# Three transfers per attention head, forget gates kept on chip, and a fifth weight buffer in a hybrid streaming block

## The chip, the cores and the metric

The kernel runs on one core of one Trainium2 chip. The metric is the device time of one execution in microseconds (us). A core has a matrix engine (TensorE, PE in the profile, its weight loads PEld), a vector engine (VectorE, DVE), an activation engine (ScalarE, ACT), a general engine (GpSimd, POOL), a queue engine that here only issues transfers (SyncE, SP), and 16 DMA engines that move the data between the chip's memory (HBM) and the on-chip SBUF. Each engine runs its own instructions strictly in order and waits for the others by semaphores.

## What is computed

One residual block over 1024 tokens of width 1024, float32 throughout. Three token mixers work on one combined projection: HGRN2, a gated linear recurrence; FoX, a forgetting attention; and cross-attention into 256 memory tokens. The branches are gated, summed and projected out; a ConvGLU feed-forward follows. Cut to the parts that the change touches:

```python
h = rmsnorm(x); z = h @ W_in              # one projection, split by columns
# HGRN2, 4 heads of 128x128
f = lb + (1 - lb) * sigmoid(f_logit)      # forget gate, per channel and token
G = cumsum(log(f)) inside chunks of 64    # the decays
# FoX, 8 heads of 64, blocks of 128 queries
s = (q . k) / 8 + Fc[t] - Fc[s]           # Fc = cumsum(log_sigmoid(f_head))
o = softmax(mask(s)) @ v
# merge
y = sum_b sigmoid(gate_b) * (branch_b @ W_b);  x += y @ W_out
x += (gelu(conv3(a)) * v) @ W_down
```

## The kernel before

**Matrix products.** Every float32 product is made of three products of a higher and a lower part (`mm3`: high x high on L122, high x low on L123, low x high on L124). Large products are split further into seven products of sums of quarter blocks, so that each weight quarter is read once ("raw" piece), summed, split into parts and used. TensorE therefore has one long queue of matmuls on 128x512 tiles.

**Stages.** The memory keys and values come first, then the token-major part of the projection in stages 0 to 4; then the column-major units. `cm_unit` (L808) is one unit: it loads four raw weight pieces of 128x512 (256 KB each, tile `ur`, 4 buffers), forms sums on GpSimd (`us`, L758), splits each operand on ScalarE (`uh`, L752) and VectorE (`ul`, L753), and multiplies in seven steps. Units 0 to 5 give the HGRN2 forget gate, query and output gate of the four heads, and units 6 to 17 the merge gates. `fill_steps` (L981) runs all units as a generator, one step at a time, and the branch projections (L860) after them.

**Attention.** `fox_attn(h)` (L1027) is one of eight heads, also a generator. `weave` (L57) runs it together with a few steps of the fill (`FOX_FILL`), so that TensorE has fill matmuls while softmax is computed elsewhere. `fox_load(h)` (L1012) loads for a head:
- `kh` and `kl`, the key's high and low part: 64 channels in rows 0 to 63 and the same again in rows 64 to 127;
- `qa`, the query: its two parts in rows 0 to 63 and rows 64 to 127;
- `nf`, two halves of the decay row, broadcast to 128 rows; and `vhl`, the values, 512 KB.

Each of kh, qa and kl comes in two transfers of 64 rows of 4 KB, from the scratch tensors `kqd`, which stage 4 stored shortly before. All of these are issued on SyncE's queue. For head h > 0 the loads may issue only after the first output store of head h-1 (`marks["head"]`, L1029 and L1094); kh, qa and kl have one buffer for each parity of the head. The logits of a block are two matmuls, qa x kh (L1046) and qa x kl (L1047); VectorE adds the decay and takes the maximum (L1052), ScalarE takes the exponential (L1062), GpSimd scales (L1064), TensorE transposes (L1075 to L1078), and the product with the values (`po`, L1087 and L1088) is folded on ScalarE and VectorE (`yp`, L1091 and L1092), which frees the output bank, and stored (L1093).

**Forget gates and decays.** `put_hg` (L787) finishes the gate of an HGRN2 head in two halves: tanh on ScalarE, clamping on GpSimd, and a store to `hgd` on GpSimd's queue (L798). `decays(h)` (L963) loads the gate of a head again (`fk`, L966), scales it into two rows (L969 and L970), takes one Ln over 128x2048 on ScalarE (L972, with a table load of its own), and runs four cumulative scans (L975) with four subtractions (L976) on VectorE; then the two results are stored (L979). Its three steps run at steps 2, 4 and 6 of units 1, 2, 4 and 5.

**Order.** The program is written in the order of these generators; a scheduler with a modelled timeline then orders each engine's instructions. `tc.high_priority(n)` lets a piece go ahead of what was written before, `tc.issue_after(x)` keeps a piece behind instruction x.

Of the kernel before, what the change touches and what calls it, by code (L numbers as in the profile page):

```python
# [9 lines left out]
F32 = mybir.dt.float32  # L10
F32R = mybir.dt.float32r
AF = mybir.ActivationFunctionType
# [19 lines left out]
FOX_FILL = [2, 6, 5, 5, 5, 5, 5, 5]  # L32
HGRN_FILL = [32, 30, 28, 22]
AHEAD = 300
STAGE_STEPS = 3
ORDER = (1, 2, 0)
UNITS = [[("f", 0), ("q", 0)], [("g", 0), ("f", 1)], [("q", 1), ("g", 1)], [("f", 2), ("q", 2)],
# [32 lines left out]
def tile_block(ctx: ExitStack, tc: tile.TileContext, xT, x_rows, memT, vec, fbias, mats, hmask, w_ff, w_tm, w_cm,  # L70
# [679 lines left out]
    def u_operand(src):  # L750
        h, l = (ur.tile([P, HB], F32R, tag=t, name=t, bufs=3) for t in ("uh", "ul"))
        marks["cast"] = S.copy(h, src)  # L752
        V.tensor_sub(l, src, h.bitcast(F32))  # L753
        return h, l

    def u_sum(a, b):
# [19 lines left out]
    def put_gate(i):  # L776
# [7 lines left out]
            S.dma_start(gd[i, n], t)  # L784
        return put

    def put_hg(what, h):  # L787
        def put(c, n, ps, e):
            t = out_tile()
            dst = hgd[h][what][:, n * HB:(n + 1) * HB]  # L790
            if what == 0:
                if e is None:
                    S.activation(t, ps, AF.Tanh, scale=-0.5)
                else:
                    combine(t, ps, e, c)
                    S.activation(t, t, AF.Tanh, scale=0.5)
                G.tensor_scalar(t, t, TMIN, TMAX, ALU.max, ALU.min)
                G.dma_start(dst, t)  # L798
                return
            else:  # L800
                z = e if e is not None else ur.tile([P, HB], F32, tag="ue", name="ue", bufs=3)
                combine(z, ps, e, c)
                S.activation(t, z, AF.Tanh, scale=0.5)
                V.scalar_tensor_tensor(out=t, in0=t, scalar=1.0, in1=z, op0=ALU.add, op1=ALU.mult)
            SP.dma_start(dst, t)
        return put

    def cm_unit(u, puts):  # L808

        x, z, y = (banks[(u + i) % 3] for i in range(3))  # L810

        def put(c, n, ps, e):
            puts[c](c, n, ps, e)

        raw = []
        for i in range(4):
            t = ur.tile([P, HB], F32, tag="ur", name="ur", bufs=4)
            SP.dma_start(t, w_cm[u, i])
            raw.append(t)
        a11, a12, a21, a22 = raw  # L820
        o1, o6 = u_operand(a11), u_operand(a12)
        s1 = u_sum(a21, a22)
        s2 = u_sum(s1, a11)
        u_product(x, o1, "B11", True)
        e1 = u_snap(x)
        yield
        u_product(z, o6, "B21", True)
        put(0, 0, z, e1)
        o3 = u_operand(s2)
# [30 lines left out]
    def branches():  # L860
# [1 line left out]
        yh, yl = ([half[k // 2][:, k % 2, :] for k in range(4)] for half in halves)  # L862

        def chunk(br, j):
            raw = ur.tile([P, HB], F32, tag="ur", name="ur", bufs=4)
            SP.dma_start(raw, w_br[br, j])
            wh, wl = u_operand(raw)
            half = [slice(n * HB, (n + 1) * HB) for n in range(2)]

            def step(ps, n, k):  # L870
                ks = slice(k * P, (k + 1) * P)
                mm3(ps, wh[:, ks], wl[:, ks], yh[k][:, half[n]], yl[k][:, half[n]], k == 0, k == 3)

            if j in (0, 7):
                ps = [ps_proj(), ps_proj()]
                for k in range(4):
                    for n in range(2):
# [84 lines left out]

    def decays(h):  # L963

        fk = pf.tile([P, 2, T], F32, tag="fk", name=f"fk_{h}")
        SP.dma_start(fk[:, 0, :], hgd[h][0])  # L966
        yield
        hc = slice(h, h + 1)
        V.tensor_scalar(fk[:, 1, :], fk[:, 0, :], nc1[:, hc], c1p[:, hc], ALU.mult, ALU.add)  # L969
        V.tensor_scalar(fk[:, 0, :], fk[:, 0, :], c1[:, hc], c0[:, hc], ALU.mult, ALU.add)  # L970
        with tc.issue_after(marks["cast"].ins):
            S.activation(fk, fk, AF.Ln)  # L972
        for n in range(4):
            sl = slice(n * 256, (n + 1) * 256)
            V.tensor_tensor_scan(fk[:, 0, sl], resets, fk[:, 0, sl], 0.0, ALU.mult, ALU.add)  # L975
            V.tensor_sub(fk[:, 1, sl], fk[:, 0, sl], fk[:, 1, sl])  # L976
        yield
        for i in range(2):
            SP.dma_start(hgd[h][3 + i], fk[:, i, :])  # L979

    def fill_steps():  # L981
        for u, spec in enumerate(UNITS):
            for i, _ in enumerate(cm_unit(u, [puts_of(*s) for s in spec])):
                if u == len(UNITS) - 1 and i == 1:
                    load_y(ORDER[0])
                if u == 3 and i == 4:
                    recurrence_masks()
                if u in (1, 2, 4, 5):
                    if i == 2:
                        steps = decays((1, 2, 4, 5).index(u))  # L990
                    if i in (2, 4, 6):
                        next(steps, None)
                yield
        yield from branches()
        ur.release()
# [10 lines left out]
    resets = pf.tile([P, 256], F32, tag="resets", name="resets")  # L1006
    SP.dma_start(resets, mats[:, 3 * P:3 * P + 256])
    mskf = pf.tile([P, P], F32, tag="mskf", name="mskf")
    with tc.high_priority(2 * AHEAD):
        SP.dma_start(mskf, mats[:, 2 * P:3 * P])  # L1010

    def fox_load(h):  # L1012
        p, a = h // 2, slice(64 * (h % 2), 64 * (h % 2) + 64)
        kh, qa, kl = (pf.tile([P, T], F32R, tag=f"{t}{h % 2}", name=f"{t}_{h}") for t in ("kh", "qa", "kl"))
        for t, (u, v) in ((kh, (0, 0)), (qa, (2, 3)), (kl, (1, 1))):
            SP.dma_start(t[0:64, :].bitcast(F32), kqd[p][u // 2][a, u % 2, :])
            SP.dma_start(t[64:128, :].bitcast(F32), kqd[p][v // 2][a, v % 2, :])
# [9 lines left out]
    def fox_attn(h):  # L1027
# [3 lines left out]
        for tp in range(4):  # L1031
            pts = []
            for j in range(2):
                tb = 2 * tp + j
                ns = (tb + 1) * P
                tsl = slice(tb * P, (tb + 1) * P)
                pt = pf.tile([P, T], F32, tag="pt", name="pt", bufs=4)
                st = small("st", 4)
                nfm = pf.tile([P, P], F32, tag="nfm", name="nfm")
                G.tensor_tensor(nfm, nf[tb // 4][:, tb % 4 * P:tb % 4 * P + P], mskf, ALU.add)  # L1040
                m = 0
                for s0 in range(0, ns, HB):
# [851 lines left out]
```

## Time and profile before

| | |
|---|---|
| median of 3 runs | 1677.19 us (1676.16 to 1678.06) |
| the profiled execution | 1679.46 us, span 1677.7 us, mean granted clock 0.998 |
| TensorE busy | 1654.1 us, 99% of the span |
| VectorE, ScalarE, GpSimd busy | 1215.9, 845.5, 441.4 us |
| moved by DMA | 298.20 MB, 178 GB/s on average |
| first load of head 0 issued | 322.28 us |
| first logits of head 0 and of head 7 | 329.62 and 627.82 us |

The span runs from the first to the last instruction of the profiled execution, and its own time is some 2 us longer. In a row of a timeline stand start, duration, engine, line and operation, the tile written and the tile read, the shapes, and in brackets how long the engine stood idle before it and what ended that. "SPq" is an instruction that issues a transfer: its time is that of the issue, not of the transfer. In a row of the waits stand the engine with tile and line that waited, what it waited for, the total in us, how often, and the longest. In a row by stretches stand the stretch, its length, the busy time of PE, PEld, DVE, ACT and POOL with the number of instructions, the granted TensorE clock (1.00 is full), the share of the 16 DMA engines in use, and GB/s. "DMA packets" counts the pieces of the transfers, with the number of those under 512 B, 2 KB and 8 KB.

### The profile page before, as it was taken

To read this page: it belongs to the slowest core of one execution; us is meant where nothing else is said; L and a number is where in the kernel's file an instruction comes from. 1 tells how busy PE (TensorE), PEld (TensorE's weight loads), DVE (VectorE), ACT (ScalarE), POOL (GpSimd) and SP (SyncE) were. 2 spreads that over 40 slices of the span, in tenths; PEclk is the share of its full clock that TensorE was granted. 3 is DMA by queue.
4 is the path that set the end of the run, shared out by engine and by line. 5 is a ranking of instruction groups with operands and counts; after the bars stand their busy time and mean duration, and the time that the engine had idled before them with its cause. 6 is when DMAs were issued, how large, how long until landed. Compare 5 with 4: busy or idle time off the path is not lost.

```text
span 1677.7 us, 24989 instructions
## 1 busy us (share of the span) xinstructions
PE 1654.1 (99%) x8915; PEld 1417.1 (84%) x8915; DVE 1215.9 (72%) x2179; ACT 845.5 (50%) x1453; POOL 441.4 (26%) x469
## 2 busy tenths in 40 slices
PE   8999999999999999999999999999999999999999
PEld 7989999777788888888888888888888888888887
DVE  7875766588786766678776868978878788675664
ACT  8655554466666565556333257544434434343332
POOL 1143543455444444223011052221111111100000
PEclk9999999999999999999999999999999999999999
DMA  7253352655455552646866899666544454394782
GB/s 283 98 189 103 130 180 107 200 191 164 157 164 154 151 157 103 200 133 217 317 183 174 253 215 224 175 190 179 146 132 126 153 149 130 133 390 150 239 283 87
DMA packets 132061, 298.20 MB, mean 178 GB/s; under 512 B 14008, under 2 KB 31672, under 8 KB 131296
## 3 DMA queue, kind: packets, MB, share of 16 engines
q1 hardware_dynamic: 100576, 210.08, 36.9%
q0 software_dynamic: 22144, 71.84, 16.8%
q10 hardware_dynamic: 9216, 14.68, 2.3%
q8 instruction: 70, 1.15, 0.3%
q14 instruction: 55, 0.45, 0.1%
HBM read 216.40 MB, written 103.22 MB: 191 GB/s over the span
## 4 chain that ended last, share of the span: by engine, by line
PE 54%; DMA 1%; DVE 0%; ACT 0%; issue 0%
PE pp L122 10%; PE pp L123 10%; PE pp L124 10%; PE lg L124 4%; PE lg L122 4%; PE lg L123 4%; PE tr L122 3%; PE tr L124 3%; PE tr L123 3%; PE po L124 1%; PE po L122 1%; PE po L123 1%; DMA yd<-hz 1%; PE lg L1194 1%; PE lg L1185 0%; PE po L1227 0%
## 5 line engine op out<-in xcount | busy, mean ns | idle before, releaser
L1374 ACT CAST wh<-s 128x512 fp32r<-128x512 f32 x84 | 51.5, 620 | 119.1 <-PE pp L123 62.5
L128 ACT CAST dwh<-wr 128x1024 fp32r<-128x1024 f32 (+1 forms) x41 | 40.2, 980 | 114.9 <-PE tr L123 39.2
L1527 POOL DMA_DIRECT2D rw<-in_w_up x40 | 21.8, 551 | 260.5 <-DVE wl L1375 165.1
L752 ACT CAST uh<-ur 128x512 fp32r<-128x512 f32 x78 | 48.2, 618 | 77.7 <-PE pp L123 67.0
L1374 ACT CAST wh<-rw 128x512 fp32r<-128x512 f32 x66 | 40.6, 622 | 77.2 <-PE pp L123 47.2
L1064 POOL TENSOR_SCALAR pt<-pt,st 128x128 f32<-128x128 f32 (+3 forms) x64 | 57.5, 900 | 57.8 <-DVE st L1063 37.9
L136 DVE TENSOR_TENSOR dwl<-wr,dwh 128x1024 fp32r<-128x1024 f32 (+1 forms) x41 | 46.3, 1129 | 34.4 <-ACT dwh L128 34.3
L1062 ACT ACTIVATE pt<-pt,st 128x128 f32<-128x128 f32 (+3 forms) x64 | 49.8, 778 | 41.7 <-DVE st L1059 36.2
L753 DVE TENSOR_TENSOR ul<-us,uh 128x512 fp32r<-128x512 f32 x72 | 54.4, 759 | 21.5 <-ACT uh L752 21.0
L122 PE MATMUL pp<-B21h,uh 128*128 128x512 f32 x168 | 66.6, 398 | 1.2 <-DVE ue L150 1.2
L753 DVE TENSOR_TENSOR ul<-ur,uh 128x512 fp32r<-128x512 f32 x78 | 62.3, 800 | 6.0 <-ACT uh L752 5.1
L124 PE MATMUL pp<-B21h,ul 128*128 128x512 f32 x168 | 66.2, 394 | 0.1
L123 PE MATMUL pp<-T2l,uh 128*128 128x512 f32 x168 | 66.3, 395 | 0.0
L758 POOL TENSOR_TENSOR us<-ur 128x512 f32<-128x512 f32 x36 | 50.9, 1413 | 58.2 <-DMA ur<-in_w_cm 44.4
L122 PE MATMUL pp<-T2h,uh 128*128 128x512 f32 x168 | 66.1, 396 | 0.0
L123 PE MATMUL pp<-B21l,uh 128*128 128x512 f32 x168 | 65.9, 392 | 0.0
L124 PE MATMUL pp<-T2h,ul 128*128 128x512 f32 x168 | 65.8, 392 | 0.0
L752 ACT CAST uh<-us 128x512 fp32r<-128x512 f32 x72 | 43.9, 615 | 37.0 <-POOL us L758 21.1
L136 DVE TENSOR_TENSOR wl<-raw,wh 128x1024 fp32r<-128x1024 f32 x29 | 40.0, 1386 | 27.5 <-ACT wh L128 27.3
L758 POOL TENSOR_TENSOR us<-us,ur 128x512 f32<-128x512 f32 x36 | 49.5, 1375 | 38.7 <-issue 33.7
L1375 DVE TENSOR_TENSOR wl<-s,wh 128x512 fp32r<-128x512 f32 x84 | 57.3, 683 | 0.9 <-ACT wh L1374 0.6
L1375 DVE TENSOR_TENSOR wl<-rw,wh 128x512 fp32r<-128x512 f32 x66 | 44.4, 686 | 15.8 <-PE pp L124 13.5
(745 smaller groups left out, 6154.5 us busy)
## 6 DMA issues: line engine op xcount, KB each, us to landing
rw<-in_w_up POOLq DMA_DIRECT2D x40, 512.0 KB, 4.8
ur<-in_w_cm SPq DMA_DIRECT2D x72, 256.0 KB, 3.7
sd<-in_w_dn POOLq DMA_DIRECT2D x30, 512.0 KB, 8.3
br<-yd SPq DMA_DIRECT2D x30, 512.0 KB, 5.1
gd<-uo ACTq DMA_DIRECT2D x48, 256.0 KB, 3.0
gt<-gd SPq DMA_DIRECT2D x48, 256.0 KB, 5.0
yd<-fc SPq DMA_DIRECT2D x44, 256.0 KB, 2.3
raw<-in_w_tm SPq DMA_DIRECT2D x20, 512.0 KB, 3.4
```

Source lines behind the costliest of these rows:

```text
L122: PE.matmul(ps, lh, rh, start=first, stop=False, skip_group_check=more)
L123: PE.matmul(ps, lh, rl, start=False, stop=False, skip_group_check=more)
L124: return PE.matmul(ps, ll, rh, start=False, stop=last, skip_group_check=more)
L128: S.copy(out, in_)
L136: return (sub or V).tensor_sub(l, src, h.bitcast(F32))
L752: marks["cast"] = S.copy(h, src)
L753: V.tensor_sub(l, src, h.bitcast(F32))
L758: G.tensor_add(t, a, b)
L1062: S.activation(pt[:, :ns], pt[:, :ns], AF.Exp, bias=st[:, 2:3], accum_out=st[:, 3:4])
L1064: G.tensor_scalar(pt[:, :ns], pt[:, :ns], st[:, 3:4], 0.0, ALU.mult, ALU.add)
L1374: late["cast"] = S.copy(h, src)
L1375: late["split"] = V.tensor_sub(l, src, h.bitcast(F32))
```

## The change

It does seven things.
1. kh, kl and qa come in one transfer each, of 128 rows: for kh and kl the source is a broadcast of 2 over 64 rows of 4 KB, for qa the two parts are the outer dimension.
2. Head 0's three transfers get a high priority, and the load of `mskf` and one store of the HGRN2 query (`stored_late`) are kept behind them.
3. The raw weight tile `ur` has 5 buffers instead of 4.
4. The forget gates of heads 2 and 3 and the first half of head 1's are written straight into the `fk` tile and neither stored nor loaded. Head 0's gate and the second half of head 1's are still stored and loaded, in halves.
5. `decays` is split into steps at the places of a table (`DECAYS`): scaling, Ln, two scans, two scans and the first half of the stores, the rest of the stores. The scans are held behind the latest VectorE split (`marks["low"]`).
6. `pt` has a tile of its own size for each place of a block pair instead of 4 buffers of full width.
7. `nfm` has 2 buffers instead of 1.

```diff
+DECAYS = {at: (h, i == 0) for h, when in enumerate(((6, 8, 9, 10, 11, 12), (14, 16, 17, 18, 19, 20), (27, 28, 29, 30, 31), (35, 36, 37, 38, 39)))
+          for i, at in enumerate(when)}
...
     def put_hg(what, h):
         def put(c, n, ps, e):
-            t = out_tile()
+            kept = what == 0 and (h > 1 or (h == 1 and n == 0))
+            if kept:
+                if h not in gates:
+                    gates[h] = gate_tile(h)
+                t = gates[h][:, 0, n * HB:(n + 1) * HB]
+            else:
+                t = out_tile()
...
-                G.dma_start(dst, t)
+                if not kept:
+                    G.dma_start(dst, t)
...
-            SP.dma_start(dst, t)
+            if (what, h, n) == (1, 0, 1):
+                stored_late.append(partial(SP.dma_start, dst, t))
+            else:
+                SP.dma_start(dst, t)
...
-            t = ur.tile([P, HB], F32, tag="ur", name="ur", bufs=4)
+            t = ur.tile([P, HB], F32, tag="ur", name="ur", bufs=5)
...
     def decays(h):
-        fk = pf.tile([P, 2, T], F32, tag="fk", name=f"fk_{h}")
-        SP.dma_start(fk[:, 0, :], hgd[h][0])
+        if h == 0:
+            gates[h] = gate_tile(h)
+        fk = gates[h]
+        half = [slice(n * HB, (n + 1) * HB) for n in range(2)]
+        for n in ((0, 1), (1,), (), ())[h]:
+            SP.dma_start(fk[:, 0, half[n]], hgd[h][0][:, half[n]])
...
-        for n in range(4):
-            sl = slice(n * 256, (n + 1) * 256)
-            V.tensor_tensor_scan(fk[:, 0, sl], resets, fk[:, 0, sl], 0.0, ALU.mult, ALU.add)
-            V.tensor_sub(fk[:, 1, sl], fk[:, 0, sl], fk[:, 1, sl])
         yield
-        for i in range(2):
-            SP.dma_start(hgd[h][3 + i], fk[:, i, :])
+        for n in range(2):
+            for sl in (slice(n * HB + i * 256, n * HB + i * 256 + 256) for i in range(2)):
+                with tc.issue_after(marks["low"].ins):
+                    V.tensor_tensor_scan(fk[:, 0, sl], resets, fk[:, 0, sl], 0.0, ALU.mult, ALU.add)
+                V.tensor_sub(fk[:, 1, sl], fk[:, 0, sl], fk[:, 1, sl])
+            if n:
+                store(0)
+            yield
+        store(1)
...
-        for t, (u, v) in ((kh, (0, 0)), (qa, (2, 3)), (kl, (1, 1))):
-            SP.dma_start(t[0:64, :].bitcast(F32), kqd[p][u // 2][a, u % 2, :])
-            SP.dma_start(t[64:128, :].bitcast(F32), kqd[p][v // 2][a, v % 2, :])
+        twice = lambda part: kqd[p][0][a, part, :].unsqueeze(0).to_broadcast([2, 64, T])
+        with nullcontext() if h else tc.high_priority(2 * AHEAD):
+            for t, src in ((kh, twice(0)), (qa, kqd[p][1][a].rearrange("a b t -> b a t")), (kl, twice(1))):
+                loaded = SP.dma_start(t.bitcast(F32), src)
+        if h == 0:
+            with tc.high_priority(2 * AHEAD), tc.issue_after(loaded.ins):
+                SP.dma_start(mskf, mats[:, 2 * P:3 * P])
+            with tc.issue_after(loaded.ins):
+                stored_late.pop()()
...
-                pt = pf.tile([P, T], F32, tag="pt", name="pt", bufs=4)
+                pt = pf.tile([P, (5 + 2 * (tp % 2) + j) * P], F32, tag=f"pt{tp % 2}{j}", name="pt")
                 st = small("st", 4)
-                nfm = pf.tile([P, P], F32, tag="nfm", name="nfm")
+                nfm = pf.tile([P, P], F32, tag="nfm", name="nfm", bufs=2)
```

Lines move by 2 to 42: L1016 and L1017 become L1054, L1046 and L1047 become L1088 and L1089, L1092 becomes L1134, L975 becomes L1011.

SyncE's queue at the loads of head 0, before (kqd is the scratch tensor with keys and queries, hgd that of the recurrence, uo an output tile of a unit):

```order
95 L655 DMA kqd_96<-ko 256x1x512
96 L805 DMA hgd_101<-uo 128x512
97 L1010 DMA mskf<-in_mats 128x128
98 L1016 DMA kh_3820<-kqd_93 64x1024
99 L1017 DMA kh_3820<-kqd_93 64x1024
100 L1016 DMA qa_3821<-kqd_93 64x1024
101 L1017 DMA qa_3821<-kqd_93 64x1024
102 L1016 DMA kl_3822<-kqd_93 64x1024
103 L1017 DMA kl_3822<-kqd_93 64x1024
104 L1020 DMA nf<-negFd 128x512 x2
105 L1022 DMA vhl<-vhd_97 128x8x128
```

The same place after the change:

```order
95 L657 DMA kqd_96<-ko 256x1x512
96 L1054 DMA kh_3818<-kqd_93 128x1x1024
97 L1054 DMA qa_3819<-kqd_93 128x1x1024
98 L1054 DMA kl_3820<-kqd_93 128x1x1024
99 L1057 DMA mskf<-in_mats 128x128
100 L1059 DMA hgd_101<-uo 128x512
101 L1062 DMA nf<-negFd 128x512 x2
102 L1064 DMA vhl<-vhd_97 128x8x128
```

The three loads moved ahead of the store and the mask; each has 128 rows on the side of SBUF.

TensorE's queue at the first logits of head 0, before (pp is the bank of a fill product, lg that of the logits):

```order
2243 L1046 MATMUL lg<-kh_3820,qa_3821 128x128
2244 L1046 MATMUL lg<-kh_3820,qa_3821 128x256
2245 L122 MATMUL pp<-T1h,uh 128x512
2246 L123 MATMUL pp<-T1l,uh 128x512
2247 L122 MATMUL pp<-T2h,uh 128x512
2248 L123 MATMUL pp<-T2l,uh 128x512
2249 L124 MATMUL pp<-T2h,ul 128x512
2250 L122 MATMUL pp<-T2h,uh 128x512
2251 L123 MATMUL pp<-T2l,uh 128x512
```

And after:

```order
2242 L126 MATMUL pp<-B21h,ul 128x512
2243 L1088 MATMUL lg<-kh_3818,qa_3819 128x128
2244 L1088 MATMUL lg<-kh_3818,qa_3819 128x256
2245 L124 MATMUL pp<-T1h,uh 128x512
2246 L125 MATMUL pp<-T1l,uh 128x512
2247 L1089 MATMUL lg<-kl_3820,qa_3819 128x128
2248 L1089 MATMUL lg<-kl_3820,qa_3819 128x256
2249 L124 MATMUL pp<-T2h,uh 128x512
```

The kl products moved up by 13 rows: they are rows 2247 and 2248 now, four behind the first kh product, and were rows 2260 and 2261.

VectorE's queue at the decays of the third recurrence head, before (fk is the gate, yp the output half of a block pair, pl the lower part of the transposed weights of the softmax):

```order
505 L969 TENSOR_SCALAR fk_5911<-fk_5911,nc_71,c1p 128x1024
506 L1063 RECIPROCAL st<-st 128x1
507 L970 TENSOR_SCALAR fk_5911<-fk_5911,c_70,c_69 128x1024
508 L753 TENSOR_TENSOR ul<-us,uh 128x512
509 L975 SCALAR_TENSOR_TENSOR fk_5911<-resets,fk_5911 128x256 x4
510 L1092 TENSOR_TENSOR yp<-po,yp 64x256
```

And the decays of the same head after:

```order
472 L1002 TENSOR_SCALAR fk_5285<-fk_5285,nc_71,c1p 128x1024
473 L1105 RECIPROCAL st<-st 128x1
474 L1003 TENSOR_SCALAR fk_5285<-fk_5285,c_70,c_69 128x1024
475 L823 SCALAR_TENSOR_TENSOR uo<-uo,ue 128x512
476 L1094 ISA pt,st<-lg,nf 128x512
477 L1094 ISA st 128x1
478 L1134 TENSOR_TENSOR yp<-po,yp 64x256
479 L1094 ISA pt,st<-lg,nf 128x384
480 L1094 ISA st 128x1
481 L1094 ISA pt,st<-lg,nfm 128x128
482 L1094 ISA st 128x1
483 L1011 SCALAR_TENSOR_TENSOR fk_5285<-resets,fk_5285 128x256 x2
```

The addition into yp stands ahead of the scans now, and the four scans, one row before, are three rows now, 483, 486 and 488, with other work between.

More of the change, by code (lines that the diff above doesn't have):

```diff
@@ L752, in u_operand @@
         marks["cast"] = S.copy(h, src)
-        V.tensor_sub(l, src, h.bitcast(F32))
+        marks["low"] = V.tensor_sub(l, src, h.bitcast(F32))
         return h, l
@@ L785, in put_gate, with gate_tile @@
         return put
+    stored_late = []
+    gates = {}
+    def gate_tile(h):
+        return pf.tile([P, 2, T], F32, tag="fk", name=f"fk_{h}")
     def put_hg(what, h):
         def put(c, n, ps, e):
-            t = out_tile()
+            kept = what == 0 and (h > 1 or (h == 1 and n == 0))
[5 more added lines that the diff above has]
+                t = out_tile()
             dst = hgd[h][what][:, n * HB:(n + 1) * HB]
             if what == 0:
-                if e is None:
+                if kept and e is not None:
+                    combine(e, ps, e, c)
+                    S.activation(t, e, AF.Tanh, scale=0.5)
+                elif e is None:
                     S.activation(t, ps, AF.Tanh, scale=-0.5)
@@ L864, in chunk @@
         def chunk(br, j):
-            raw = ur.tile([P, HB], F32, tag="ur", name="ur", bufs=4)
+            raw = ur.tile([P, HB], F32, tag="ur", name="ur", bufs=5)
             SP.dma_start(raw, w_br[br, j])
@@ L963, in decays, with store @@
     def decays(h):
-        fk = pf.tile([P, 2, T], F32, tag="fk", name=f"fk_{h}")
-        SP.dma_start(fk[:, 0, :], hgd[h][0])
+        if h == 0:
[4 more added lines that the diff above has]
+            SP.dma_start(fk[:, 0, half[n]], hgd[h][0][:, half[n]])
+        if h < 2:
+            yield
+        hc = slice(h, h + 1)
+        def store(n):
+            for i in range(2):
+                SP.dma_start(hgd[h][3 + i][:, half[n]], fk[:, i, half[n]])
+        with tc.issue_after(marks["low"].ins):
+            V.tensor_scalar(fk[:, 1, :], fk[:, 0, :], nc1[:, hc], c1p[:, hc], ALU.mult, ALU.add)
+        V.tensor_scalar(fk[:, 0, :], fk[:, 0, :], c1[:, hc], c0[:, hc], ALU.mult, ALU.add)
         yield
-        hc = slice(h, h + 1)
-        V.tensor_scalar(fk[:, 1, :], fk[:, 0, :], nc1[:, hc], c1p[:, hc], ALU.mult, ALU.add)
-        V.tensor_scalar(fk[:, 0, :], fk[:, 0, :], c1[:, hc], c0[:, hc], ALU.mult, ALU.add)
         with tc.issue_after(marks["cast"].ins):
             S.activation(fk, fk, AF.Ln)
-        for n in range(4):
-            sl = slice(n * 256, (n + 1) * 256)
-            V.tensor_tensor_scan(fk[:, 0, sl], resets, fk[:, 0, sl], 0.0, ALU.mult, ALU.add)
-            V.tensor_sub(fk[:, 1, sl], fk[:, 0, sl], fk[:, 1, sl])
         yield
-        for i in range(2):
-            SP.dma_start(hgd[h][3 + i], fk[:, i, :])
+        for n in range(2):
+            for sl in (slice(n * HB + i * 256, n * HB + i * 256 + 256) for i in range(2)):
+                with tc.issue_after(marks["low"].ins):
+                    V.tensor_tensor_scan(fk[:, 0, sl], resets, fk[:, 0, sl], 0.0, ALU.mult, ALU.add)
+                V.tensor_sub(fk[:, 1, sl], fk[:, 0, sl], fk[:, 1, sl])
+            if n:
+                store(0)
+            yield
+        store(1)
     def fill_steps():
@@ L987, in fill_steps @@
                     recurrence_masks()
[L988 to L992, printed above, removed]
+                at = 7 * u + i
+                if at in DECAYS:
+                    h, begin = DECAYS[at]
+                    if begin:
+                        steps = decays(h)
+                    next(steps, None)
                 yield
@@ L1008, in tile_block @@
     mskf = pf.tile([P, P], F32, tag="mskf", name="mskf")
-    with tc.high_priority(2 * AHEAD):
-        SP.dma_start(mskf, mats[:, 2 * P:3 * P])
     def fox_load(h):
```

## The prediction

> **What bounds the kernel now.** The page first, for which engine fills the span.
>
> ```profile
> span 1677.7 us, 24989 instructions
> PE 1654.1 (99%) x8915; PEld 1417.1 (84%) x8915; DVE 1215.9 (72%) x2179; ACT 845.5 (50%) x1453; POOL 441.4 (26%) x469
> ```
>
> TensorE is busy for 99% of the span and the change leaves its matmuls alone, so all there is to win is its idle time, some 24 us, and what it loses at a low clock. All there is to lose is new idle time. The list of waits says where the idle time is; these are the rows of the stage that the change touches (attention woven with the column units, from about 320 us).
>
> ```profile
> engine line waited for: us in total, times, longest us
> PE po L1087 <- DVE yp L1092: 3.4, 1, 3.4
> PE lg L1047 <- DMA kl<-kqd: 1.8, 2, 1.0
> ...
> PE lg L1046 <- DMA qa<-kqd: 1.6, 1, 1.6
> ...
> PE tr L1075 <- POOL pt L1064: 0.5, 1, 0.5
> ```
>
> So 3.4 us in two or three waits for the head loads, and one wait of 3.4 us for VectorE. Of that last one the timelines of VectorE, ScalarE and TensorE tell the cause, read in this order.
>
> ```profile
> 425.13 1.28 ACT L972 ACT_TABLE_LOAD   x1
> 427.50 1.92 ACT L972 ACTIVATE fk<-fk 128x2048 f32<-128x2048 f32 x1 [1.08 <-DVE fk L970]
> ...
> 429.44 2.44 DVE L975 TENSOR_TENSOR_SCAN fk<-resets,fk 128x256 f32<-128x256 f32 x4 [1.38 <-ACT fk L972]
> 431.80 0.39 DVE L1092 TENSOR_TENSOR yp<-po,yp 64x256 f32<-64x256 f32 x1
> ...
> 432.34 0.55 PE L1087 MATMUL po<-ph,vhl 128*128 128x256 f32 x1 [3.41 <-DVE yp L1092]
> 432.69 0.63 PE L122 MATMUL pp<-B22h,uh 128*128 128x512 f32 x1
> 433.12 0.63 PE L123 MATMUL pp<-B22l,uh 128*128 128x512 f32 x1
> ```
>
> VectorE stood still 1.38 us for the Ln, then ran four scans, and the small addition that frees the output bank was queued behind them. The two matmuls after it start 0.43 us apart; elsewhere the same form starts 0.23 us apart (below). The table by stretches has the clock.
>
> ```profile
> 430.90:437.80 6.90, 5.46 (x14) 4.35 (x14) 5.63 (x12) 3.57 (x7) 1.12 (x1) 0.51 0.54 197
> 437.80:441.00 3.20, 3.20 (x22) 2.92 (x21) 3.00 (x7) 2.09 (x4) 2.60 (x3) 1.00 0.04 14
> ```
>
> At 0.51 from 430.9 to 437.8 us, the restart at 432.34 is followed by 5.4 us at half clock: 2.7 us lost on top of the 3.4. A long stall costs about 2.7 us more than its length here.
>
> **Part 1: the head loads.** Three transfers of 128 rows take the place of six of 64 rows, eight times. SyncE's timeline at head 1 has the old issue times, and TensorE's has the first use.
>
> ```profile
> 357.49 0.55 SPq L1016 DMA_DIRECT2D kh<-kqd  x1
> ...
> 360.00 0.59 SPq L1016 DMA_DIRECT2D kl<-kqd  x1
> 360.63 0.60 SPq L1017 DMA_DIRECT2D kl<-kqd  x1
> ...
> 367.28 0.30 PE L1047 MATMUL lg<-kl,qa 128*128 128x128 f32 x1 [0.96 <-DMA kl<-kqd]
> ```
>
> What the new transfers take is the disputed price. The new source of kh and kl is a leading dimension of 2 with stride zero over 64 rows of 4 KB, that of qa 2 by 64 rows with a real stride; the built program carries these patterns as [2, 64, 1024], while every old half had 64 in front. Two transfers of the trace show how many of the 16 DMA engines take part: a store of 8 rows alone in its window, and a load of 128 rows alone in its own.
>
> ```profile
> DMA packets 16, 0.03 MB, mean 9 GB/s; under 512 B 8, under 2 KB 8, under 8 KB 16
> ffd<-ff SPq DMA_DIRECT2D x1, 32.0 KB
> ```
> ```profile
> GB/s 0 0 0 0 0 0 0 0 0 0 0 0 164 131 33 66 66 33 33 66 131 328 360 426 426 393 426 360 459 295 1 0 0 0 0 0 0 0 0 0
> DMA packets 144, 0.26 MB, mean 105 GB/s; under 512 B 16, under 2 KB 16, under 8 KB 144
> ...
> ur<-in_w_cm SPq DMA_DIRECT2D x1, 256.0 KB
> ```
>
> Beside its data packets each transfer has packets under 512 B, one for each engine that reports its end: 16 for the 128 rows, 8 for the 8 rows. The trace thus bears out that the slowest dimension caps the number of engines at 8 when it is 8. It can't tell that from "8 packets, so at most 8 engines", since the eight rows were one packet each; no row has few rows in front and many packets. I take the cap to hold for 2 as well: two engines move each of the 24 transfers, one for each half.
>
> The Trainium skill speaks against this edit as much as for it. "DMA: Bandwidth & Descriptors", section "Rules for kernel authors", says that two transfers to disjoint halves of the partitions share the same engines and should be one of 128 partitions, which would make every load quicker. The same table warns that an outermost dimension smaller than 16, a leading zero-stride broadcast by name, holds the whole transfer to that many engines; this trace agrees as far as its 8-row store goes. By the first rule alone the sum would be rival A's, by the second it is the forecast's.
>
> The price of two engines: the best slices of the 128-row load moved 426 GB/s, 26.6 GB/s for each of 16. On two engines 524,288 bytes take 9.9 us, and three in a row on one queue 29.6 us. Ahead of that comes what a load takes before its data moves:
>
> ```profile
> ur<-in_w_cm SPq DMA_DIRECT2D x72, 256.0 KB, 3.7
> ```
>
> 256 KB at 426 GB/s are 0.6 of these 3.7 us, which leaves 3.1. So kl lands 32.7 us after kh's issue. Spread over 16 engines it would be 3 x 1.24 + 3.1 = 6.8 us. The old six took 2.5 us from kh's issue to kl's, 0.6 more to its second half, and then
>
> ```profile
> DMA to landing us min/median/max: 5.8/6.4/7.4
> ```
>
> 9.5 us in all (this last row is that of tile kl).
>
> How long TensorE can go on without them: kh's issue to the first matmul with kl was 9.8 us at head 1 (rows above, 0.96 of it idle) and 10.6 us at head 7:
>
> ```profile
> 617.24 0.55 SPq L1016 DMA_DIRECT2D kh<-kqd  x1
> ...
> 627.88 0.28 PE L1047 MATMUL lg<-kl,qa 128*128 128x128 f32 x1
> ```
>
> For heads 1 to 7, read in the same way and without the idle time, it was 8.8, 8.8, 12.9, 12.9, 10.0, 10.7 and 10.6 us. The new order puts more matmuls between the output product that frees the loads and the first kl product; counted in the two orders at 0.23 us each, 6.2, 0.2, 1.5, 2.9, 3.8, 0.5 and 0.9 us more. That makes 15.0, 9.0, 14.4, 15.8, 13.8, 11.2 and 11.5. At head 0 the loads no longer stand behind a store and the mask:
>
> ```profile
> 319.44 0.52 SPq L655 DMA_DIRECT2D kqd<-ko  x1
> 321.42 0.33 SPq L805 DMA_DIRECT2D hgd<-uo  x1
> 321.81 0.42 SPq L1010 DMA_DIRECT2D mskf<-in_mats  x1
> 322.28 0.52 SPq L1016 DMA_DIRECT2D kh<-kqd  x1
> ...
> 327.68 0.39 PE L124 MATMUL pp<-B21h,ul 128*128 128x512 f32 x1
> 329.62 0.47 PE L1046 MATMUL lg<-kh,qa 128*128 128x128 f32 x2 [1.55 <-DMA qa<-kqd]
> 329.93 0.40 PE L122 MATMUL pp<-T1h,uh 128*128 128x512 f32 x1
> ```
>
> They can issue at about 320.0. Without the 1.55 us TensorE is at the kh logits at 328.07, and four rows on, where the new order has kl's, at 328.7: 8.7 us. The eight leads add up to 99.4 us, so eight times 32.7 less 99.4 is **162 us of stalls** (24 at head 0, 17 to 24 at the others). Each is long enough for the half clock: 8 x 2.7 = **22 us**. Nothing covers these: TensorE runs its queue in order, its fill matmuls stand behind the logits, and ScalarE, VectorE and GpSimd have nothing to do without TensorE.
>
> Behind the loads on SyncE's queue stand nf, vhl and the next weight pieces; on the two busy engines they come after kl. From 0 (hidden beside the logits) to 3 us per head (nf and vhl, 1 MB at 426 GB/s, are 2.5 us), I take 2: **16 us**. The worst end is higher: if TensorE needs a piece issued behind the loads before it reaches the logits, the lead that is left is lost too, 50 us if that takes half of all leads. What the stalls replace are the 1.55, 0.96 and 0.85 us of waits for the loads.
>
> **Part 2: decays in steps, gates kept.** The wait of 3.41 us goes: in the new order the output addition stands ahead of the scans, which come two, one and one with other work between. With the half clock it is 6.1 us. Kept gates save ten times 256 KB of stores and loads, for which TensorE did not wait: nothing. Steps after a mark can be late: the table loads of 1.28 us around each Ln still stand in ScalarE's queue, and a gate kept in the one fk buffer makes ScalarE's Tanh wait for the preceding head's last store. From -6.1 to +6.1 (a stall of the same kind elsewhere); I take -6.1, since the row that named the cause is gone.
>
> **Part 3: fifth raw piece, two nfm, pt cut to size.** One TensorE wait names them (POOL pt, 0.5 us, in the list above): nothing, -0.5 at best, and +1 if a store of the extra pieces crowds the loads.
>
> **The sum** against the profiled execution, 1679.5 us (span 1677.7): 162 + 22 + 16 - 3.4 - 6.1 = +190.5, so 1870. The median of the three runs shown is 2.3 lower; against it, **1867.7**.
>
> **The rivals.**
> A. *All 16 engines take part* (the sign is the other one). Then kl lands 6.8 us after kh's issue, less than any of the eight leads (8.7 to 15.8), no wait for a load is left, and -3.4 - 6.1 = -9.5: **1667.7** (1664 to 1675, the dearer end if a stall for Ln comes back in part). It decides at the number of engines: with a lead of 8.7 to 15.8 us less 3.1, three transfers must move in 5.6 to 12.7 us, which takes 5 to 11 engines. For it: the halves as carried hold 128 packets of 4 KB, enough for 16. Against: no row has more engines than its slowest dimension.
> B. *Loads spread, but the decays only move.* Of the 9.5 us the 3.4 stay won and one or two stalls of 6.1 us come elsewhere: 1677.2 - 3.4 = **1673.8** up to 1680. For it: the scans now stand in eight steps instead of four blocks, each with its own chance of being in front of something. Against: of the four blocks only one shows in the waits.
> C. *Two engines, but a gate queues behind them*: a weight piece needed ahead of the logits, as priced above: up to **1918**. It is the forecast's upper part, not a case of its own.
>
> **How the numbers follow.** About 0.2%, 3.4 us, is what a measurement of this kernel can tell from no change. The cap on engines decides nearly everything. The one row that bears on it stands on the forecast's side without proving it; I give the cap 0.74, A 0.20, B 0.06. A is faster throughout, B half within 0.2% and the rest about even: faster 0.22, same 0.03, slower 0.75. The forecast's own range is 1815 to 1945: down if nf and vhl are hidden (-16), the clock costs half (-11) and leads are 3 us longer (-24); up by the 50 us of C and by packets at the mean of the busy slices (388 GB/s over those from 328 to the second 360: 1.0 us per transfer, +23). Cases of both signs hold the chance, so for 8 in 10 the range reaches down to A: 1666 to 1945, leaving out some 0.15.
>
> **What would show it.** Right: in the changed profile kh, qa and kl land some 13, 23 and 33 us after the first issue, the waits list has TensorE's lg rows for DMA kl at eight times and 17 to 24 us, the slices from 320 to 800 us show the DMA share falling to about 1 or 2 tenths inside each stall, and the completion packets number 2 for each transfer. Wrong: 16 small packets for a load, kl landing 5 to 7 us after its issue, and no lg wait over 1 us. Part 2 is wrong if a po or lg row still waits over 1 us for yp or for an fk row; part 1's leads are wrong if TensorE stops ahead of the logits for a cast of a weight piece.

## The result and the profile after

The changed kernel takes 1875.5 us (median of four runs, 1873.74 to 1877.35), the kernel before 1677.62 (four runs, 1676.16 to 1680.31): ratio 1.1174, 95% interval 1.116 to 1.1188, slower by 198 us. The forecast was 1867.7.

The page of the changed kernel has the loss in its first lines, and in the slices from the eighth to the eighteenth where the attention runs.

```profile
span 1875.6 us, 24956 instructions
PE 1674.5 (89%) x8915; PEld 1433.4 (76%) x8915; DVE 1210.7 (65%) x2179; ACT 845.5 (45%) x1453; POOL 437.5 (23%) x464
PE   9999999448659656849999999999999999999999
PEclk9999999679779778879999999999999999999999
DMA  7154433332332322222559669975664444376682
```

TensorE is idle for 201 us of the span instead of 24 (+177.5) and "busy" for 1674.5 us instead of 1654.1 (+20.4) with the same 8915 matmuls: the second number is the low clock. Where the idle time is, the list of TensorE's waits says.

```profile
PE lg L1088 <- DMA qa<-kqd: 88.8, 7, 16.1
PE lg L1089 <- DMA kl<-kqd: 59.4, 6, 10.6
PE lg L1088 <- DVE st L1094: 25.9, 1, 25.9
PE tr L1117 <- POOL pt L1106: 11.6, 1, 11.6
```

These four rows are 185.7 us: eight heads with 20.1 to 25.9 us each. The wait for yp of 3.4 us is gone; the loads are late at every head.

How late, and on how many engines, is seen at head 0. First SyncE's queue (start, length of the issue), then the DMA view of 8 us in which nothing moves but the end of kh and most of qa, one behind the other.

```profile
319.78 0.56 SPq L1054 DMA_DIRECT2D kh<-kqd  x1
320.39 0.89 SPq L1054 DMA_DIRECT2D qa<-kqd  x1
321.32 9.49 SPq L1054 DMA_DIRECT2D kl<-kqd  x1
330.86 9.72 SPq L1057 DMA_DIRECT2D mskf<-in_mats  x1
```
```profile
DMA packets 106, 0.43 MB, mean 53 GB/s; under 512 B 2, under 2 KB 2, under 8 KB 106
q1 hardware_dynamic: 106, 0.43, 12.9%
```

53 GB/s and 12.9% of 16 engines are two engines at full speed, and two packets under 512 B report the end of the transfer that finishes in this window, kh (the load of 128 rows before the change had 16). qa, whose two parts lie a real stride apart, is as slow as kh, whose rows are repeated. At 53 GB/s 512 KB take 9.9 us. The table by stretches shows what that does to TensorE.

```profile
327.90:344.00 16.10, 0.00 (x0) 0.00 (x0) 0.00 (x0) 0.00 (x0) 0.14 (x1) 0.57 0.19 73
344.00:345.60 1.60, 1.57 (x4) 0.93 (x4) 0.00 (x0) 0.00 (x0) 0.00 (x0) 0.50 0.78 253
345.60:354.80 9.20, 0.05 (x1) 0.00 (x0) 0.00 (x0) 0.00 (x0) 0.00 (x0) 0.50 0.39 126
354.80:361.00 6.20, 6.09 (x16) 4.88 (x17) 4.09 (x14) 3.44 (x9) 4.59 (x6) 0.52 0.63 214
```

For 16.1 us no engine works, then TensorE gets qa and does four matmuls at half clock, stands again for kl, and goes on at half clock. In the rows of SyncE there is something that the prediction did not have: the issue of kl itself takes 9.49 us and that of the small mask 9.72. I read this as SyncE standing at an issue while the queues of the two engines are full; whatever the reason, everything behind it on SyncE is issued late.

### The profile page after: what moved, and what is told of

Read it like the earlier page. It is cut to its first block, busy times and chain, and to the rows that moved or that the text cites. A ratio compares the mean times of both kernels' runs of the same rounds, so it can differ in the third digit from the quotient of the medians.

```text
span 1875.6 us, 24956 instructions
## 1 busy us (share of the span) xinstructions
PE 1674.5 (89%) x8915; PEld 1433.4 (76%) x8915; DVE 1210.7 (65%) x2179; ACT 845.5 (45%) x1453; POOL 437.5 (23%) x464
## 5 line engine op out<-in xcount | busy, mean ns | idle before, releaser
L1088 PE MATMUL lg<-kh,qa 128*128 128x512 f32 (+2 forms) x96 | 36.5, 383 | 114.7 <-DMA qa<-kqd 88.8
L1088 PEld LDWEIGHTS lg<-kh,qa 128*128 128x128 f32 x96 | 19.8, 207 | 120.0 <-issue 91.1
L1082 POOL TENSOR_TENSOR nfm<-nf,mskf 128x128 f32<-128x128 f32 x64 | 33.4, 530 | 270.6 <-DMA nf<-negFd 223.3
L1089 PE MATMUL lg<-kl,qa 128*128 128x512 f32 (+2 forms) x96 | 35.4, 376 | 59.4 <-DMA kl<-kqd 59.4
L138 DVE TENSOR_TENSOR dwl<-wr,dwh 128x1024 fp32r<-128x1024 f32 (+1 forms) x41 | 46.3, 1130 | 34.5 <-ACT dwh L130 34.3
L1089 PEld LDWEIGHTS lg<-kl,qa 128*128 128x128 f32 x96 | 19.9, 209 | 63.5 <-DMA kl<-kqd 61.0
L760 POOL TENSOR_TENSOR us<-us,ur 128x512 f32<-128x512 f32 x36 | 53.4, 1483 | 62.6 <-issue 52.1
```

What stands on the lines that cost most here:

```text
L138: return (sub or V).tensor_sub(l, src, h.bitcast(F32))
L760: G.tensor_add(t, a, b)
L1088: PE.matmul(ps[:, :w], qa[:, tsl], kh[:, s0:s0 + w], start=True, stop=False)
L1089: PE.matmul(ps[:, :w], qa[:, tsl], kl[:, s0:s0 + w], start=False, stop=True)
```

## The experiments

The theory on test: the count in front of the pattern is the number of engines, two here; that makes the loads late, and the lateness is the loss. Rivals: another part of the change costs the time; reading the same rows twice is slow as such; two busy engines cost time even when the loads are not late. A run of the kernel before stands beside each run; it was at 1678.3 us (e1 to e4), 1679.0 (e5 to e8), 1677.4 (e9, e10) and 1678.2 (e11, e12).

### Which part costs the time: e1 and e2

e1, the change without its first point:

```diff
-            for t, src in ((kh, twice(0)), (qa, kqd[p][1][a].rearrange("a b t -> b a t")), (kl, twice(1))):
-                loaded = SP.dma_start(t.bitcast(F32), src)
+            for t, (u, v) in ((kh, (0, 0)), (qa, (2, 3)), (kl, (1, 1))):
+                SP.dma_start(t[0:64, :].bitcast(F32), kqd[p][u // 2][a, u % 2, :])
+                loaded = SP.dma_start(t[64:128, :].bitcast(F32), kqd[p][v // 2][a, v % 2, :])
```

> The changed kernel with the head loads as they were, six transfers of 64 rows per head, all else as changed (head 0's still ahead of the store). Theory (two rows in front hold each transfer to two engines, and that alone costs the time): kl lands 6 to 8 us after its issue, no TensorE wait for qa or kl over 1 us, 1664 to 1675 us. Rival (the new order with its decay steps, or the fifth weight piece, costs the time): stays above 1850 us.

Measured: 1679.56 us, ratio 1.0009 (1.0 to 1.0019). The loss is gone, so the loads carry it. But the time is outside the 1664 to 1675 that I expected: the 9.5 us that the rest was to win are missing as well. e9, e10 and e12 look for them.

e2, the first point alone in the kernel before, at the old place on SyncE's queue:

```diff
-        for t, (u, v) in ((kh, (0, 0)), (qa, (2, 3)), (kl, (1, 1))):
-            SP.dma_start(t[0:64, :].bitcast(F32), kqd[p][u // 2][a, u % 2, :])
-            SP.dma_start(t[64:128, :].bitcast(F32), kqd[p][v // 2][a, v % 2, :])
+        for t, src in ((kh, twice(0)), (qa, kqd[p][1][a].rearrange("a b t -> b a t")), (kl, twice(1))):
+            SP.dma_start(t.bitcast(F32), src)
```

> The kernel before with only its head loads changed to three transfers, at the old place behind the store. Theory: kl lands some 34 us after kh's issue as in the changed kernel, with shorter leads (84 us over the eight heads instead of 99), so about 200 us of stalls and 20 us of low clock: 1880 to 1915 us, slower than the changed kernel. Rival (the other parts cost the time): 1670 to 1680 us.

Measured: 1872.65 us, ratio 1.1161 (1.1146 to 1.1175). The loads alone cost as much as the whole change. That this would be slower than the whole change was wrong: its stalls add up to 173 us by TensorE's timeline where about 200 had been expected. The new loads had made the scheduler place the logits anew: counted in the two traces, from the last output product ahead of kh's issue, heads 1 to 7 have some 50 more matmuls in front of their first kl product than in the kernel before, some 12 us at 0.23 us each. kl landed 33 to 36 us after kh's issue.

### Is it the count in front: e5, e6 and e4

e5 and e6 keep place, bytes and packets, and change only the pattern: c copies of 128/c rows, with c = 4 and c = 16. What arrives are not the right keys and queries. The edit of e6:

```diff
-        twice = lambda part: kqd[p][0][a, part, :].unsqueeze(0).to_broadcast([2, 64, T])
+        a = slice(a.start, a.start + 8)
+        some = lambda what, part: kqd[p][what][a, part, :].unsqueeze(0).to_broadcast([16, 8, T])
...
-            for t, src in ((kh, twice(0)), (qa, kqd[p][1][a].rearrange("a b t -> b a t")), (kl, twice(1))):
+            for t, src in ((kh, some(0, 0)), (qa, some(1, 0)), (kl, some(0, 1))):
```

> The changed kernel, with every head load read as 4 x 32 rows (a broadcast of 4 over the first 32 rows) in place of 2 x 64; bytes, packets and place in the program stay, the keys and queries that arrive are not the right ones. Theory (the count in front is the number of engines): 512 KB on 4 engines take 4.9 us, kl lands some 18 us after kh's issue; stalls of 2 to 9 us, 44 in all, and up to 16 us of low clock: 1720 to 1750 us. Rival (repeated reads of the same rows are slow as such): as the changed kernel or slower, 1870 us.

> The same with 16 x 8 rows: each row is read 16 times, and the keys and queries are not the right ones. Theory: all 16 engines, 1.2 us a transfer, kl lands 7 us after kh's issue, as fast as six halves: 1675 to 1682 us. Rival (repeated reads are slow as such): the more rows repeat, the slower, over 1875 us.

Measured, one run each: 1768.56 us with 4 in front, 1678.93 with 16. So 2, 4, 16 in front are +198, +90 and 0 us beside the kernel before. Reading each row 16 times costs nothing, and the count in front decides. In a DMA view of e5 in which kh alone moves (323 to 326 us), the busy share is that of four engines of 16:

```profile
DMA packets 61, 0.25 MB, mean 83 GB/s; under 512 B 0, under 2 KB 0, under 8 KB 61
q1 hardware_dynamic: 61, 0.25, 25.8%
```

e5 was dearer than its 1720 to 1750: kl landed 21.6 us after kh's issue at head 0, not 18, and the waits have more than the loads.

```profile
PE lg L1090 <- DMA kl<-kqd: 29.5, 6, 6.0
PE lg L1089 <- DMA qa<-kqd: 25.6, 6, 8.7
PE lg L1089 <- DMA ur<-in_w_cm: 13.9, 1, 13.9
PE tr L1118 <- POOL pt L1107: 7.1, 1, 7.1
```

A weight piece that stood behind the loads cost 13.9 us at one head.

e4 keeps the idea of fewer and larger transfers, with 64 rows of 8 KB in front: kh and kl lie beside each other in kqd and come as one tile.

```diff
+            khl = pf.tile([P, 2, T], F32R, tag=f"khl{h % 2}", name=f"khl_{h}")
+            for b in range(2):
+                SP.dma_start(khl[64 * b:64 * b + 64].bitcast(F32), kqd[p][0][a])
+            for b in range(2):
+                loaded = SP.dma_start(qa[64 * b:64 * b + 64, :].bitcast(F32), kqd[p][1][a, b, :])
+            kh, kl = khl[:, 0, :], khl[:, 1, :]
```

> The changed kernel, with kh and kl in one tile: two transfers of 64 rows of 8 KB (512 KB each, 64 in front) carry both, and qa comes in two halves of 64 rows: four transfers per head, the same bytes. Theory (the count in front decides, not the number or size of the transfers): all 16 engines, kl lands under 10 us after the first issue, 1664 to 1675 us, within 3 us of the six loads. Rival (large transfers of repeated rows are slow as such): stalls of over 5 us per head, above 1710 us.

Measured: 1679.52 us, ratio 1.0007 (0.9999 to 1.0016), the same as e1 and like it over its range, by 4.5 us. Transfers of 512 KB are not slow: these landed 6.0 us after their issue (median). With 64 rows in front, fewer transfers win nothing here either.

### From late loads to lost time: e3, e11, e7 and e8

e3 issues the three transfers some 40 us earlier, behind the first logits of the head before.

```diff
-        with tc.issue_after(marks["head"].ins) if h else nullcontext():
-            kh, kl, qa, vhl, nf = fox_load(h)
...
+                    if tb == 0 and h < 7:
+                        with tc.issue_after(logits.ins):
+                            fox_keys(h + 1)
```

> The changed kernel, with each head's three transfers issued as soon as the head before has made its first logits (some 40 us earlier) instead of after its first output store; nf and vhl stay. Theory (the stall is landing time less lead): the waits of heads 1 to 7 for qa and kl go, head 0 keeps its 24 us, and the queue's other loads may wait up to 30 us behind head 1's: 1695 to 1735 us. Rival (transfers on two engines cost time whenever they run, by blocking the queue or slowing others): above 1800 us.

Measured: 1841.73 us, ratio 1.0984 (1.0961 to 1.1006). The theory as I had it fell: "stall = landing less lead" would have left head 0 alone. The waits of the seven other heads for qa and kl are indeed gone, and others took their place.

```profile
PE tr L1128 <- POOL pt L1117: 35.3, 2, 17.8
PE po L1140 <- DVE yp L1145: 33.5, 2, 18.1
PE tr L1128 <- DVE pl L138: 22.5, 2, 21.0
PE pp L124 <- DVE uo L150: 20.4, 1, 20.4
PE lg L1096 <- DMA qa<-kqd: 16.2, 1, 16.2
```

One of them read through: SyncE's queue first, then ScalarE, VectorE and TensorE as they release each other.

```profile
414.70 9.20 SPq L1054 DMA_DIRECT2D kl<-kqd  x1
424.01 10.74 SPq L999 DMA_DIRECT2D hgd<-fk  x2
...
439.81 2.39 SPq L827 DMA_DIRECT2D hgd<-uo  x2
```
```profile
451.36 0.63 ACT L822 ACTIVATE uo<-ue 128x512 f32<-128x512 f32 x1 [19.04 <-DMA hgd<-uo]
452.02 0.37 ACT L1144 COPY yp<-po 64x256 f32<-64x256 f32 x1
452.63 0.41 DVE L1145 TENSOR_TENSOR yp<-po,yp 64x256 f32<-64x256 f32 x1
453.19 0.55 PE L1140 MATMUL po<-ph,vhl 128*128 128x256 f32 x1 [15.40 <-DVE yp L1145]
```

From 414.70 to 442.20 SyncE stands at one issue after another, so the stores of two output tiles of the units (uo) are issued only from 439.81 on. ScalarE stands 19.04 us until such a store has landed and the tile is free again. Its copy out of the bank po is queued behind that, VectorE's addition behind the copy, and TensorE, which needs the bank, goes on at 453.19. The loads were in time, and the queue that issued them was not.

e11 keeps them early but alone: kh, qa and kl of heads 2 to 7 each behind another output store, some 12 us apart; heads 0 and 1 by halves.

```diff
+            with tc.issue_after(stores[4 * (h - 2) + n + 1].ins):
+                SP.dma_start(t.bitcast(F32), src)
```

> The kernel of e1, with heads 2 to 7 loaded by three transfers with two rows in front again, each issued alone and early: kh behind the second output store of two heads before, qa behind its third, kl behind its fourth, some 12 us apart; heads 0 and 1 by halves. So no more than about one of them is in the two engines' queues at a time. Theory (in e3 the time was lost because the queues of the two engines were full and SyncE stood at the next issue): issues stay under 1 us, the other loads wait up to 10 us behind one transfer and have more slack than that, no stall over 3 us at heads 2 to 7: 1680 to 1695 us. Rival (two busy engines hold up every other transfer enough to stop TensorE): 5 to 10 us at each of six heads, 1715 to 1750 us.

Measured: 1726.24 us, ratio 1.0288 (1.0274 to 1.0302). The issues of these loads are short now, and of all others only three are left over 1.5 us (9.4 us together).

```profile
L1070 SPq DMA_DIRECT2D kh<-kqd x6: 523/530/572, 366.7 to 621.8; - x6
...
L1070 SPq DMA_DIRECT2D kl<-kqd x6: 523/524/530, 397.8 to 647.8; - x6
```

Still 46.7 us over e1 for six heads, inside the rival's range and not the theory's. GpSimd's timeline tells why: weight pieces that were issued right behind such a load.

```profile
601.61 1.26 POOL L760 TENSOR_TENSOR us<-ur 128x512 f32<-128x512 f32 x1 [15.25 <-DMA ur<-in_w_cm]
...
604.90 1.26 POOL L1125 TENSOR_SCALAR pt<-pt,st 128x384 f32<-128x384 f32 x2
```

qa was issued at 585.3 and the pieces from 586.4 on; the first was usable at 601.6. GpSimd waited 15.25 us for it, and the scaling of pt, for which TensorE then stood 8.7 us, was queued behind. Over the run GpSimd waits 95.1 us for weight pieces (47.8 in e1), and TensorE 26.3 us for pt (2.0 in e1); at half clock behind such stalls TensorE is busy 15.7 us longer than in e1. The two make 40 of the 46.7 us. So the two engines cost in three ways: the load is late, SyncE stands at full queues, and every other transfer of the same queue waits behind the load on those two engines. e11 takes the first two nearly away and keeps a third of the loss per head (46.7 us at six heads, 7.8 each, against 196 us at eight, 24.5 each).

e7 puts the three transfers of the changed kernel on GpSimd's queue, and e8 does so with e3's early issue:

```diff
-                loaded = SP.dma_start(t.bitcast(F32), src)
+                loaded = G.dma_start(t.bitcast(F32), src)
```

> The changed kernel, with each head's three transfers issued on GpSimd's queue instead of SyncE's. In the changed kernel SyncE's issue of kl took 9 us and what stood behind was issued late. Theory 1 (two engines for each transfer, the same two in turn): kl lands as late, stalls as before less the nf and vhl that come late: 1840 to 1870 us. Theory 2 (this queue hands out other engines to each transfer): the three run side by side, kl lands some 13 us after issue, 1685 to 1710 us. Rival (the queue does not matter): 1870 to 1880 us.

> The early issue of e3 (a head's loads behind the first logits of the head before), on GpSimd's queue. Theory (in e3 the loads were in time, and TensorE waited for output stores, weight pieces and gates that stood behind the blocked issue on SyncE's queue): with SyncE free these come in time, and only head 0's stall is left: 1685 to 1715 us. Rival (what was lost in e3 was the busy DMA engines, not the blocked queue): 1800 to 1845 us, as e3.

Measured, one run each: 1897.15 and 1893.17 us. Both were outside every expectation. GpSimd's timeline of e7:

```profile
339.98 0.82 POOL L1054 DMA_DIRECT2D qa<-kqd  x1 [15.69 <-issue]
353.22 0.78 POOL L1054 DMA_DIRECT2D kl<-kqd  x1 [12.43 <-issue]
```

GpSimd starts such an issue only every 13 us and does nothing in between; qa lands 13.0 us after its issue (median), about when the next one starts. Here the standing engine is one that TensorE needs, for nfm and pt: its waits for pt are 116 us in e7. So e8 could not tell a blocked queue from busy engines; that was left to e11.

### The gain that did not come: e9, e10 and e12

e9 is the kernel before with the fourth and fifth point of the change alone (kept gates, decays in steps); e10 is e1 with these two undone. The core of the edit in e9, which e10 has the other way round:

```diff
-                if u in (1, 2, 4, 5):
-                    if i == 2:
-                        steps = decays((1, 2, 4, 5).index(u))
-                    if i in (2, 4, 6):
-                        next(steps, None)
+                at = 7 * u + i
+                if at in DECAYS:
+                    h, begin = DECAYS[at]
+                    if begin:
+                        steps = decays(h)
+                    next(steps, None)
```

> The kernel before with only the kept gates and the decays in steps; six head loads, four raw pieces, pt and nfm as before. Theory (the stall of 3.4 us only moves: the scans no longer hold yp, but table load, Ln and table load, 4.5 us in a row on ScalarE, hold a copy that TensorE needs): no wait for yp over 1 us, a new wait of 1 to 3 us for ue or uh, 1674 to 1681 us. Rival (the decays win their 6 us and the rest of the change gives them back): 1669 to 1673 us.

> The kernel of e1 (six loads, head 0's ahead of the store, five raw pieces, pt and nfm as changed) with gates and decays as in the kernel before. Theory: the wait for yp of 3.4 us or one like it is still there, the waits for loads are within 1 us of before: 1674 to 1681 us. Rival (the rest loses what the decays win): 1681 to 1687 us.

Measured: 1683.93 us, ratio 1.0042 (1.003 to 1.0054), and 1681.33 us, ratio 1.0023 (1.0013 to 1.0033). Either part alone is a little slower than the kernel before, both together (e1) are within 0.2% of it. The time of e9 is above both of its ranges, that of e10 on the border between its two. In e9 no wait for yp over 1 us is left, as expected, and TensorE has a new one of 3.6 us for pt, which stands behind the Ln: ScalarE was right, the tile (ue or uh) was not. That wait does not explain all of the 6.5 us that e9 loses to the kernel before, and the rest was not followed up. In e10 TensorE waits 2.3 us for pl, which stands behind the four scans.

In e1 the same happens at another copy. ScalarE and TensorE of e1:

```profile
362.74 1.28 ACT L1006 ACT_TABLE_LOAD   x1
364.04 1.92 ACT L1006 ACTIVATE fk<-fk 128x2048 f32<-128x2048 f32 x1
365.97 1.28 ACT L1104 ACT_TABLE_LOAD   x1
367.27 1.04 ACT L1104 ACTIVATE pt<-pt,st 128x896 f32<-128x896 f32 x1
...
368.93 0.58 ACT L765 COPY ue<-pp 128x512 f32<-128x512 f32 x1
```
```profile
369.57 0.50 PE L124 MATMUL pp<-T3h,uh 128*128 128x512 f32 x1 [2.66 <-ACT ue L765]
```

Table load, Ln, table load: 4.5 us in a row, and the copy that frees TensorE's bank is behind them.

e12 is e1 with this Ln behind the latest copy into ue:

```diff
-        S.copy(e, ps)
+        marks["snap"] = S.copy(e, ps)
...
-        with tc.issue_after(marks["cast"].ins):
+        with tc.issue_after(marks["snap" if h == 1 else "cast"].ins):
             S.activation(fk, fk, AF.Ln)
```

> The kernel of e1, with the Ln of the second recurrence head issued behind ScalarE's latest copy into ue instead of its latest cast. Theory (what e1 lost again was this Ln with its two table loads, 4.5 us in front of the ue copy that TensorE waited 2.66 us for): that wait and its half clock go, 1673 to 1677 us. Rival (the order of this stage has such a wait somewhere in every variant): another wait of 1 to 3 us comes up and it stays at 1677 to 1683 us.

Measured: 1679.49 us, ratio 1.0007 (0.9996 to 1.0017): the rival's range. The wait of 2.66 us is gone, and another of 2.28 us has come 7 us later, at the logits, with the scans that now run there on VectorE.

```profile
371.24 2.90 DVE L1011 TENSOR_TENSOR_SCAN fk<-resets,fk 128x256 f32<-128x256 f32 x3
374.06 1.42 DVE L1012 TENSOR_TENSOR fk<-fk 128x256 f32<-128x256 f32 x1
```

No version beat the kernel before. Whether the stage can be ordered without such a wait was not settled; in five orders of it (before, e1, e9, e10, e12) it has one of 2.3 to 3.6 us.

## Why the prediction was right, point by point

- **Two engines for each transfer: right.** 53 GB/s, 12.9% of the engines, two completion packets; e5 and e6 show that the count in front sets it (+198, +90, 0 us with 2, 4 and 16). The rate was read from slices of 426 GB/s, called the best though one stood at 459; two engines at 53 GB/s are 26.5 each, as 426 over 16 had given. The rule of the Trainium skill on outermost dimensions under 16 ("DMA: Bandwidth & Descriptors", section "Rules for kernel authors"), which the 8-row store could only suggest, holds in this kernel with these numbers. Its other rule, one transfer of 128 partitions in place of two halves, gains nothing measurable here: e1, e4 and e6 are within 0.2% of the kernel before.
- **Landing of kl 32.7 us after kh's issue: right, 1.8 us short of the mean.** At the six heads where TensorE's wait ended on it, it was 33.2 to 35.3 us, mean 34.5. qa, forecast at 23, came after 24.2 at head 0.
- **Stalls of 162 us and 16 more for what is behind: 178 forecast, 185.7 measured.** 24 us at head 0 were 25.4. By the sum's own terms, with 34.5 for all eight heads, the later landing makes 14 us more than the 162, and TensorE got 9 us less far before it stopped (276 us of landing less 185.7 are 90, not 99).
- **Low clock, 22 us: 20.4 measured.** This is the changed kernel's busy time less that of the kernel before; each also has some 7 us at half clock away from the late loads, which cancel in the difference. The fourth row of the table by stretches has it at work, 0.52 for 6.2 us after the stall.
- **"The decays win 6.1 us and the waits for the loads 3.4": near in number here, wrong as a gain of the change.** The named wait did go, and beside the four rows above the changed kernel has 15.4 us of idle time where the kernel before has 23.6. But e1 shows the change without its new loads at 0 to +3.2 us. The sum took "the row that named the cause is gone" for a gain, while Ln and its table loads stood in the same queues of the same full stage: this is what rival B said, with 0.06 too low a chance, and not only where the loads are spread. Why the term came near its number in the changed kernel and not in e1 is not shown (stalls of 20 us at each head may hide what would otherwise move), so that agreement is luck. The total of +190.5 missed +198 by 7.4 us: 7.7 more of stalls, 1.6 less of low clock, 1.3 less won.
- **Rival C, something queued behind the loads: it came, in a stronger form.** The prediction let nf, vhl and weight pieces wait in the engines' queues for 0 to 3 us per head. In truth SyncE itself stood still: between 318 and 900 us it has 24 issues of over 1.5 us, 227 us together, and the kernel before has one, of 1.8 us. Head 1 of the changed kernel shows the chain: the gate that is still reloaded stood behind the loads, VectorE behind the gate, the logits behind VectorE.

```profile
386.82 9.71 SPq L1062 DMA_DIRECT2D nf<-negFd  x1
396.57 1.06 SPq L1064 DMA_DIRECT2D vhl<-vhd  x1
397.73 9.94 SPq L827 DMA_DIRECT2D hgd<-uo  x1
407.76 0.38 SPq L992 DMA_DIRECT2D fk<-hgd  x1
```
```profile
414.15 0.81 DVE L1002 TENSOR_SCALAR fk<-fk,nc,c1p 128x1024 f32<-128x1024 f32 x1 [26.94 <-DMA fk<-hgd]
414.87 0.68 DVE L1094 CUSTOM_DVE_ANT_0 pt<-lg,nf 128x512 f32<-128x512 f32 x1
```

TensorE stopped there at 389.7, ahead of the logits that need kh, and went on at 415.6. The forecast's number for that head, 17.7 us, was 8 short, the largest miss of the eight. By the prediction's own sign (a row of logits that waits over 1 us for yp or an fk row) part 2 is wrong here too, through the half of a gate that is still stored and loaded. That a full queue holds the issuing engine was in no row of the kernel before, where each issue of a head's keys and queries took 0.5 to 0.6 us; e3, e7 and e8 were missed for the same reason.

## What to carry to other kernels

Before merging transfers, look at the first dimension of the pattern as the instruction carries it, on the side of the source too: a broadcast of two in front of 64 rows turned sixteen DMA engines into two and cost nearly 12%, and a different split of the same bytes (16 in front) cost nothing. Issuing a late transfer earlier repairs it only in part if it shares its queue with others (34 of 198 us in e3; in e11, one transfer at a time, all but 7.8 of 24.5 us a head): ask what stands behind it, and on which in-order engine. When the row that named a stall is gone, the stall need not be: the work that caused it stayed in the same full stage here, and in four orders of it the stall came back under another name.

## What the runs showed of the hardware

- SyncE's issue of a third 512 KB transfer on the two engines took 9.49 us and ended at 330.8, 2.8 us before the two packets that report the end of the first (9.9 us of data); with 4 in front all three were issued in 0.5 to 0.8 us and the next small load took 3.38 us. These rows fit an issue that waits for room in the queues of the engines that it uses; the queues themselves are in no view. All that follows on SyncE waited with it.
- GpSimd started such a transfer only every 13 us, and did no other work in between. The data then moved at 49 GB/s, about what two engines moved on SyncE's queue (53), so on this queue, too, the transfer was not spread.

```profile
342.00:352.00 10.00, 0.00 (x0) 0.00 (x0) 0.00 (x0) 0.00 (x0) 0.00 (x0) 0.50 0.14 49
```

- The half clock after a stall did not grow with the stall's length: after 20 to 26 us in which TensorE stood, the granted clock was back at 1.00 some 3.2 to 5.8 us after the last restart of a head; after the stall of 3.4 us in the kernel before it took 5.5 us. The eight heads cost 20.4 us of busy time together, 2.6 us each, against 2.7.
